# Grouped output norms of four recurrent mixers: row sums from ScalarE squares, and one reciprocal-root chain per unit

## The chip, the cores and the metric

The kernel runs on one core of a Trainium2 chip. The metric is the device time of one execution in microseconds. The engines are called as the profile calls them: PE (TensorE, matrix products), DVE (VectorE), ACT (ScalarE), POOL (GpSimd), and SP, which issues most DMAs. PSUM is the memory into which PE writes, SBUF the memory of the tiles.

## The reference

One layer of a decoder trunk on 2048 tokens of width 1024, in float32:

```
u = rmsnorm(x, norm_w);  proj = u @ w_in            # one projection for all mixers
y_a = gla(...)      # 4 heads, q and k of width 64, values of 128
y_b = mlstm(...)    # 4 heads of width 128
y_c = hgrn2(...)    # 4 heads of width 128
y_d = ssd(...)      # 8 heads of width 64, in 2 groups of 256
h = x + concat(y_a, y_b, y_c, y_d) @ w_out;  out = rmsnorm(h, final_norm_w)

grouped_rmsnorm(o) = o * rsqrt(mean(o*o over the group) + eps) * w    # ends each mixer
gla, hgrn2:  grouped_rmsnorm(o, per head) * silu(z)
mlstm:       grouped_rmsnorm(sigmoid(o_raw) * h, per head) * silu(z)
ssd:         grouped_rmsnorm(y * silu(z), 2 groups)
```

All four mixers are causal recurrences, computed in chunks. The change touches only how the last step of each mixer, the grouped norm with its gate, is computed.

## The kernel before

The tokens are worked through in two halves of 1024, and a half is eight chunks of 128 tokens, tiled with a chunk's tokens on the 128 partitions. In each half ten units follow one another: two pairs of GLA heads, two SSD groups, four HGRN2 heads and two pairs of mLSTM heads. After both halves a last stage multiplies by w_out.

Every unit has two parts. First its projections: `ps_c` (channels on the partitions) and `ps_t` (tokens on the partitions), both made in three matmuls of a split into a high and a low part (`uh`, `ul`, `hi`, `lo`). Then the recurrence, in a chain of dependent steps. For GLA and HGRN2 (`lin_unit`) these are decay levels, each of which multiplies `kb` and `qf` by a decay on DVE (L496, L497) and makes scores on PE (`ps_s`); then, for each of two groups of four chunks (`for g in range(2)`), a transpose of the keys (`ps_kt`, L567), its copy by ACT to SBUF (L569), the state update (`ps_u`, then DVE L577), and the output (`ps_o`). In SSD the recurrence steps chunk by chunk (L876 to L899). mLSTM has the same steps as the linear units, with exponentials made on ACT (L749, L757).

The Tile framework decides the order: each engine executes its instructions in one fixed order, which a list scheduler made at build time, and waits on semaphores. The scheduler puts matmuls of the following unit's projections (`ps_c`, `ps_t`) between the dependent steps of the recurrence. How many of them stand at a place is what this text calls the cover there.

Weights are loaded some groups ahead. `load_w` makes the high part on ACT (L228) and the low part on POOL (L230), two POOL instructions for a weight group. There are two buffers of each part, so the POOL pair starts when PE has done with the group before last.

The end of a unit before the change is, for each group of chunks and each head: ACT copies `ps_o` to SBUF (L590), ACT squares the copy (L602), DVE sums the rows (L604), eleven small DVE instructions form a reciprocal root with three Newton steps (`rsqrt`, L129), four DVE instructions multiply by the root and the gate `sz` (L595), DVE transposes (L613) and four DMAs store. SSD has its own version in `finish(g)`: squares with row sums in one ACT instruction (L843, with `accum_out`), the root, four scalings (L850); `finish(0)` is called in the middle of the chunk loop, after chunk 4.

The tile pool `t2k` (five buffers of 2 KB a partition) holds most intermediate tiles of this work; `small` holds the per-row factors.

Of the kernel before, what the change touches and what calls it, by code (L numbers as in the profile page):

```python
# [10 lines left out]
F32 = mybir.dt.float32  # L11
# [4 lines left out]
AF = mybir.ActivationFunctionType  # L16
ALU = mybir.AluOpType
# [4 lines left out]
P = 128  # L22
# [94 lines left out]
class Kernel:  # L117
# [11 lines left out]
    def rsqrt(self, x, w):  # L129

        nc, sm = self.nc, self.small
        y = sm.tile([P, 8], F32, tag="rs_y", name="rs_y")[:, :w]
        t = sm.tile([P, 8], F32, tag="rs_t", name="rs_t")[:, :w]
        nc.vector.tensor_scalar(out=t.bitcast(I32), in0=x.bitcast(I32), scalar1=1, scalar2=None, op0=ALU.logical_shift_right)
        nc.vector.tensor_scalar(out=y.bitcast(I32), in0=t.bitcast(I32), scalar1=-1.0, scalar2=float(0x5F3759DF), op0=ALU.mult, op1=ALU.add)
        for _ in range(3):
            nc.vector.scalar_tensor_tensor(out=t, in0=x, scalar=-0.5, in1=y, op0=ALU.mult, op1=ALU.mult)
            nc.vector.tensor_tensor(t, t, y, op=ALU.mult)
            nc.vector.scalar_tensor_tensor(out=y, in0=t, scalar=1.5, in1=y, op0=ALU.add, op1=ALU.mult)
        return y  # L140
# [276 lines left out]
    def lin_unit(self, nh, f, kb, qp, v, sz, car, eps, ycol, vt=None):  # L417
# [143 lines left out]
        if nh == 1:  # L561
            kr = flip_odd()
        for g in range(2):
            pt = self.psp.tile([P, 4, P], F32, tag="t", name="ps_kt")
# [23 lines left out]
            for h, po in enumerate(pos):  # L588
                ob = self.t2k().rearrange("p (c d) -> p c d", c=4)
                nc.scalar.copy(ob, po)  # L590
                rs2 = self.rs2[:, 4 * g:4 * g + 4]
                fac = self.rms(ob, eps, rs2)
                nc.vector.tensor_tensor(fac, fac, rs2, op=ALU.mult)
                for c in range(4):
                    nc.vector.scalar_tensor_tensor(out=ob[:, c], in0=ob[:, c], scalar=fac[:, c:c + 1], in1=sz(h, g)[:, c], op0=ALU.mult, op1=ALU.mult)  # L595
                self.store(ob, g, ycol + h * P)

    def rms(self, ob, eps, fac2):

        nc = self.nc  # L600
        sq = self.t2k().rearrange("p (c d) -> p c d", c=4)
        nc.scalar.activation(sq, ob, AF.Square)  # L602
        ss = self.small.tile([P, 8], F32, tag="f_ss", name="f_ss")[:, :4]
        nc.vector.tensor_reduce(out=ss, in_=sq, axis=AX.X, op=ALU.add)  # L604
        nc.vector.tensor_tensor(ss, ss, fac2, op=ALU.mult)
        nc.vector.tensor_scalar(out=ss, in0=ss, scalar1=1.0 / ob.shape[2], scalar2=eps, op0=ALU.mult, op1=ALU.add)
        return self.rsqrt(ss, 4)

# [114 lines left out]
    def mlstm(self, h):  # L723
# [17 lines left out]
        N = P + 1  # L741
        fac = self.small.tile([P, 8], F32, tag="m_fac", name="m_fac")
        for g in range(2):
            gs = slice(4 * g, 4 * g + 4)
# [32 lines left out]
            for u in range(2):  # L777
# [6 lines left out]
                nc.scalar.activation(rd[:, 2 * u:2 * u + 2].unsqueeze(2), po[:, :, P:N], AF.Abs)  # L784
            nc.vector.tensor_tensor(rd, rd, self.thr[:, gs, h], op=ALU.max)
            nc.vector.reciprocal(rd, rd)
            G = to[:, gs]
            nc.vector.scalar_tensor_tensor(out=G, in0=G, scalar=1.0, in1=ob, op0=ALU.add, op1=ALU.mult)
            rd2 = self.small.tile([P, 8], F32, tag="m_rd2", name="m_rd2")[:, :4]
            nc.vector.tensor_tensor(rd2, rd, rd, op=ALU.mult)  # L790
            nc.vector.tensor_tensor(rd, rd, self.rs[:, gs], op=ALU.mult)
            nc.vector.tensor_tensor(rd, rd, self.rms(G, 4 * EPS, rd2), op=ALU.mult)
        return to, fac
# [24 lines left out]
    def ssd(self, q):  # L818
# [18 lines left out]
        dD = self.dd[:, h4].unsqueeze(2).to_broadcast([P, 4, 64])  # L837
        def finish(g):
            yb = szs[g]
            ss = self.small.tile([P, 8], F32, tag="s_ss", name="s_ss")[:, :4]  # L840
            junk = self.t2k()[:, :256]
            for c in range(4):
                nc.scalar.activation(junk, yb[:, c], AF.Square, accum_out=ss[:, c:c + 1])  # L843
            gs = slice(4 * g, 4 * g + 4)
            nc.vector.tensor_tensor(ss, ss, self.rs2[:, gs], op=ALU.mult)
            nc.vector.tensor_scalar(out=ss, in0=ss, scalar1=1.0 / 256, scalar2=256 * EPS, op0=ALU.mult, op1=ALU.add)
            rs = self.rsqrt(ss, 4)
            nc.vector.tensor_tensor(rs, rs, self.rs[:, gs], op=ALU.mult)
            for c in range(4):
                nc.vector.tensor_scalar(out=yb[:, c], in0=yb[:, c], scalar1=rs[:, c:c + 1], scalar2=None, op0=ALU.mult)  # L850
            for j in range(2):
                self.store(yb[:, :, j * P:(j + 1) * P], g, 1536 + 256 * q + j * P)

        for g in range(2):
            yb = szs[g]
            for u in range(2):
# [3 lines left out]
                for j in range(2):  # L860
# [38 lines left out]
                    nc.vector.tensor_tensor(H, H, pu, op=ALU.add)  # L899
                    if cc == 4:  # L900
                        finish(0)
        finish(1)


# [239 lines left out]
```

## Time and profile before

| | |
|---|---|
| median of three runs | 2236.55 us (2234.35 to 2238.48) |
| the profiled execution | 2236.62 us, span 2234.8 us |
| PE busy | 2113.7 us, 95% |
| DVE busy | 1395.2 us, 62% |
| ACT busy | 821.5 us, 37% |
| POOL busy | 382.7 us, 17% |
| mean granted clock of PE | 0.983 |

A row of the timeline gives the start, the duration, the engine and the line, then the output and input tiles with their shapes, a count, and in brackets the idle time of the engine just before with the instruction that ended it. Releasers are inferred: when the one named had long been done, it was another.

### The profile page before, as it was taken

The numbers are of one execution on the slowest core, as the hardware profiler recorded it, in microseconds if no ns is written. First come the engines' busy times: TensorE is split into PE (matmuls) and PEld (weight loads), VectorE is DVE, ScalarE is ACT, GpSimd is POOL, SyncE is SP. The second block draws the span as 40 slices with busy tenths as digits, with TensorE's granted clock in tenths as the row PEclk, the third lists the DMA queues.
The fourth block names the chain that finished last, engine by engine and source line by source line (L and its number), as shares of the span: only waits on it lengthen the run. The fifth ranks groups of instructions, "written<-read, shape, count | busy, mean of one in ns | idle before, by whom it ended". The sixth has DMA issues, their size and how long they took to land.

```text
span 2234.8 us, 35049 instructions
## 1 busy us (share of the span) xinstructions
PE 2113.7 (95%) x13758; PEld 1888.7 (85%) x13758; DVE 1395.2 (62%) x3325; ACT 821.5 (37%) x1763; POOL 382.7 (17%) x283
## 2 busy tenths in 40 slices
PE   8899999989999999998989899999999999999998
PEld 7888788878889998997978788888899998788887
DVE  3674878767667676636677876776676566532332
ACT  6633332344434334454323223443343334321211
POOL 3212122320111111121211222211111210000000
PEclk9999999999999999999999989999999999999999
DMA  7111212221111132420202222211121215432321
GB/s 235 56 34 44 58 47 66 69 48 48 49 49 39 49 84 106 126 75 22 58 24 62 69 46 76 54 36 43 45 76 49 56 48 175 160 111 78 113 71 48
DMA packets 186149, 156.66 MB, mean 70 GB/s; under 512 B 141944, under 2 KB 154344, under 8 KB 178688
## 3 DMA queue, kind: packets, MB, share of 16 engines
q1 hardware_dynamic: 179504, 135.02, 21.2%
q10 hardware_dynamic: 6480, 19.40, 2.4%
q8 instruction: 108, 1.77, 0.3%
q14 instruction: 57, 0.47, 0.1%
HBM read 129.11 MB, written 25.27 MB: 69 GB/s over the span
## 4 chain that ended last, share of the span: by engine, by line
PE 75%; DVE 16%; ACT 4%; DMA 2%; issue 2%; POOL 0%; SPq 0%; ACTq 0%; DVEq 0%
PE ps_t L123 26%; PE ps_c L123 19%; PE ps_out L123 15%; PE ps_o L123 6%; PE ps_s L123 4%; PE ps_u L123 2%; PE ps_g L123 2%; DVE t2k L884 2%; DVE kb L496 2%; DVE qf L497 1%; DVE xc L717 1%; DMA ST<-w_out 1%; DMA t2k<-xT 1%; DVE st L766 1%; DMA ab<-rows 1%
## 5 line engine op out<-in xcount | busy, mean ns | idle before, releaser
L123 PE MATMUL ps_t<-hi,uh 128*128 128x256 f32 x1920 | 546.5, 285 | 0.0
L123 PE MATMUL ps_t<-hi,ul 128*128 128x256 f32 x1920 | 546.0, 284 | 0.0
L123 PE MATMUL ps_t<-lo,uh 128*128 128x256 f32 x1920 | 545.1, 284 | 0.0
L230 POOL TENSOR_TENSOR lo<-raw,hi 128x1024 fp32r<-128x1024 f32 (+1 forms) x118 | 294.4, 2515 | 950.2 <-ACT hi L228 917.3
L123 PEld LDWEIGHTS ps_t<-lo,uh 128*128 128x128 f32 x1920 | 369.8, 193 | 0.9
L123 PEld LDWEIGHTS ps_t<-hi,uh 128*128 128x128 f32 x1920 | 369.6, 193 | 1.0
L123 PEld LDWEIGHTS ps_t<-hi,ul 128*128 128x128 f32 x1920 | 369.5, 192 | 1.0 <-issue 0.9
L123 PE MATMUL ps_c<-uh,hi 128*128 128x512 f32 x896 | 357.9, 400 | 7.4 <-ACT uh L155 7.4
L123 PE MATMUL ps_c<-uh,lo 128*128 128x512 f32 x896 | 358.6, 400 | 0.0
L123 PE MATMUL ps_c<-ul,hi 128*128 128x512 f32 x896 | 357.7, 399 | 0.0
L123 PEld LDWEIGHTS ps_c<-uh,hi 128*128 128x128 f32 x896 | 171.5, 191 | 40.4 <-ACT uh L155 7.8
L123 PEld LDWEIGHTS ps_c<-ul,hi 128*128 128x128 f32 x896 | 171.6, 191 | 34.7 <-DVE ul L156 0.5
L123 PEld LDWEIGHTS ps_c<-uh,lo 128*128 128x128 f32 x896 | 171.1, 191 | 33.5
L228 ACT CAST hi<-raw 128x512 fp32r<-128x512 f32 (+1 forms) x236 | 134.6, 626 | 59.6 <-issue 33.2
L956 DVE TENSOR_TENSOR o_sz<-o_sz,ps_out 128x512 f32<-128x512 f32 (+1 forms) x33 | 22.1, 671 | 130.5 <-PE ps_out L123 127.9
L123 PE MATMUL ps_out<-woh,o_qp 128*128 128x512 f32 x288 | 94.0, 394 | 0.0
L281 ACT ACTIVATE v<-ps_t,ss 128x128 f32<-128x128 f32 x128 | 39.7, 361 | 129.3 <-PE ps_t L123 129.0
L276 ACT ACTIVATE sz<-ps_t,ss 128x128 f32<-128x128 f32 (+1 forms) x160 | 53.2, 387 | 65.2 <-PE ps_t L123 58.1
L123 PE MATMUL ps_out<-woh,o_v 128*128 128x512 f32 (+1 forms) x213 | 75.4, 389 | 0.0
L277 DVE SCALAR_TENSOR_TENSOR sz<-sz,ps_t 128x256 f32<-128x256 f32 (+1 forms) x80 | 37.5, 469 | 60.7 <-ACT sz L276 60.4
L497 DVE TENSOR_TENSOR qf<-qf,pl 128x512 f32<-128x512 f32 x72 | 61.0, 847 | 21.6 <-ACT t2k L472 12.1
L496 DVE TENSOR_TENSOR kb<-kb,pl 128x512 f32<-128x512 f32 x72 | 67.9, 942 | 10.3 <-PE ps_s L123 9.4
(367 smaller groups left out, 3793.1 us busy)
## 6 DMA issues: line engine op xcount, KB each, us to landing
raw<-w SPq DMA_DIRECT2D x59, 1024.0 KB, 4.8
y<-t2k SPq DMA_DIRECT2D x256, 64.0 KB, 2.0
t2k<-y SPq DMA_DIRECT2D x64, 256.0 KB, 3.5
t2k<-xT SPq DMA_DIRECT2D x32, 256.0 KB, 3.6
ab<-rows SPq DMA_DIRECT2D x16, 512.0 KB, 5.0
o_sz<-x ACTq DMA_DIRECT2D x16, 512.0 KB, 4.5
o_f<-x SPq DMA_DIRECT2D x12, 512.0 KB, 5.3
mb<-rows SPq DMA_DIRECT2D x8, 512.0 KB, 3.6
```

Of the source, the lines that this page charges most:

```text
L123: self.nc.tensor.matmul(out, l, r, start=start, stop=stop, skip_group_check=shared)
L228: nc.scalar.copy(hi[:, k0:k1], raw[:, k0:k1])
L230: nc.gpsimd.tensor_tensor(lo[:, k0:k1], raw[:, k0:k1], hi[:, k0:k1].bitcast(F32), op=ALU.subtract)
L276: nc.scalar.activation(out[:, j], ps[:, j], AF.Tanh, scale=self.rsh[:, t + j:t + j + 1])
L277: nc.vector.scalar_tensor_tensor(out=out, in0=out, scalar=1.0, in1=ps, op0=ALU.add, op1=ALU.mult)
L281: self.nc.scalar.activation(out[:, j], ps[:, j], AF.Identity, scale=sc[:, t + j:t + j + 1])
L496: nc.vector.tensor_tensor(kv[:, :, 0], kv[:, :, 0], pv[:, :, 1:2].to_broadcast([P, n, b]), op=ALU.mult)
L497: nc.vector.tensor_tensor(qv[:, :, 1], qv[:, :, 1], pv[:, :, 0:1].to_broadcast([P, n, b]), op=ALU.mult)
L717: nc.vector.scalar_tensor_tensor(out=acc, in0=raw[:, k:k + TH], scalar=cw[k], in1=acc, op0=ALU.mult, op1=ALU.add)
L766: nc.vector.tensor_copy(st[:, 0, :N], car)
L884: nc.vector.scalar_tensor_tensor(out=L[:, h], in0=ab[:, h, j * C:(j + 1) * C], scalar=self.acs[:, cc, 4 * q + h:4 * q + h + 1], in1=self.c ...
L956: nc.vector.tensor_tensor(xt[:, ns], xt[:, ns], ps, op=ALU.add)
```

## The change

In the linear units `squares` reads `ps_o` in PSUM with four ACT instructions, each of which squares the 128 columns of a chunk and writes their row sum into `ss`. One DVE instruction multiplies the gate tile `sz` by `ps_o`, and with that `ps_o` is free. When both groups are through, one root chain serves all eight chunks of all heads of the unit (8 or 16 columns instead of 4), and `scale_rows` multiplies each chunk by its factor. The copy L590, the square L602, the reduction L604 and the four multiplications by root and gate L595 are gone. mLSTM keeps its gated tile `G`, takes its row sums with `squares`, and makes all factors once per head. SSD calls `squares` after each group and `finish` once, after both; the call in the middle of its chunk loop is gone.

```diff
--- before.py
+++ after.py
@@ -129,8 +129,8 @@
     def rsqrt(self, x, w):
 
         nc, sm = self.nc, self.small
-        y = sm.tile([P, 8], F32, tag="rs_y", name="rs_y")[:, :w]
-        t = sm.tile([P, 8], F32, tag="rs_t", name="rs_t")[:, :w]
+        y = sm.tile([P, 16], F32, tag="rs_y", name="rs_y")[:, :w]
+        t = sm.tile([P, 16], F32, tag="rs_t", name="rs_t", bufs=1)[:, :w]
         nc.vector.tensor_scalar(out=t.bitcast(I32), in0=x.bitcast(I32), scalar1=1, scalar2=None, op0=ALU.logical_shift_right)
         nc.vector.tensor_scalar(out=y.bitcast(I32), in0=t.bitcast(I32), scalar1=-1.0, scalar2=float(0x5F3759DF), op0=ALU.mult, op1=ALU.add)
         for _ in range(3):
@@ -560,6 +560,7 @@
                     nc.scalar.copy(ST[0:64, :, 64:128], ps[0:64])
         if nh == 1:
             kr = flip_odd()
+        ss = self.small.tile([P, 16], F32, tag="f_ss", name="f_ss")[:, :8 * nh]
         for g in range(2):
             pt = self.psp.tile([P, 4, P], F32, tag="t", name="ps_kt")
             for c in range(4):
@@ -586,25 +587,33 @@
                 for h, po in enumerate(pos):
                     self.mm(po[:, c], qf[rows[h], cc * C:(cc + 1) * C], st[rows[h], c, :P], start=False, stop=c == 3, shared=True)
             for h, po in enumerate(pos):
-                ob = self.t2k().rearrange("p (c d) -> p c d", c=4)
-                nc.scalar.copy(ob, po)
-                rs2 = self.rs2[:, 4 * g:4 * g + 4]
-                fac = self.rms(ob, eps, rs2)
-                nc.vector.tensor_tensor(fac, fac, rs2, op=ALU.mult)
-                for c in range(4):
-                    nc.vector.scalar_tensor_tensor(out=ob[:, c], in0=ob[:, c], scalar=fac[:, c:c + 1], in1=sz(h, g)[:, c], op0=ALU.mult, op1=ALU.mult)
-                self.store(ob, g, ycol + h * P)
-
-    def rms(self, ob, eps, fac2):
-
-        nc = self.nc
-        sq = self.t2k().rearrange("p (c d) -> p c d", c=4)
-        nc.scalar.activation(sq, ob, AF.Square)
-        ss = self.small.tile([P, 8], F32, tag="f_ss", name="f_ss")[:, :4]
-        nc.vector.tensor_reduce(out=ss, in_=sq, axis=AX.X, op=ALU.add)
-        nc.vector.tensor_tensor(ss, ss, fac2, op=ALU.mult)
-        nc.vector.tensor_scalar(out=ss, in0=ss, scalar1=1.0 / ob.shape[2], scalar2=eps, op0=ALU.mult, op1=ALU.add)
-        return self.rsqrt(ss, 4)
+                self.squares(po, ss[:, 8 * h + 4 * g:8 * h + 4 * g + 4])
+                nc.vector.tensor_tensor(sz(h, g), sz(h, g), po, op=ALU.mult)
+        fac = self.rms(ss, P, eps, self.rs2, nh)
+        f3 = fac.rearrange("p (h c) -> p h c", h=nh)
+        nc.vector.tensor_tensor(f3, f3, self.rs2[:, None].to_broadcast([P, nh, NC]), op=ALU.mult)
+        for g in range(2):
+            for h in range(nh):
+                self.scale_rows(sz(h, g), fac[:, 8 * h + 4 * g:8 * h + 4 * g + 4])
+                self.store(sz(h, g), g, ycol + h * P)
+
+    def squares(self, ob, ss):
+
+        junk = self.t2k()[:, :ob.shape[2]]
+        for c in range(4):
+            self.nc.scalar.activation(junk, ob[:, c], AF.Square, accum_out=ss[:, c:c + 1])
+
+    def scale_rows(self, ob, fac):
+        for c in range(4):
+            self.nc.vector.tensor_scalar(out=ob[:, c], in0=ob[:, c], scalar1=fac[:, c:c + 1], scalar2=None, op0=ALU.mult)
+
+    def rms(self, ss, n, eps, fac2, nh=1):
+
+        nc = self.nc
+        s3 = ss.rearrange("p (h c) -> p h c", h=nh)
+        nc.vector.tensor_tensor(s3, s3, fac2[:, None].to_broadcast([P, nh, NC]), op=ALU.mult)
+        nc.vector.tensor_scalar(out=ss, in0=ss, scalar1=1.0 / n, scalar2=eps, op0=ALU.mult, op1=ALU.add)
+        return self.rsqrt(ss, 8 * nh)
 
     def store(self, ob, g, ycol):
 
@@ -740,6 +749,7 @@
         nc.sync.dma_start(mb, self.rows[h:h + 1, :].broadcast_to([P, TH]))
         N = P + 1
         fac = self.small.tile([P, 8], F32, tag="m_fac", name="m_fac")
+        ss = self.small.tile([P, 16], F32, tag="f_ss", name="f_ss")[:, :8]
         for g in range(2):
             gs = slice(4 * g, 4 * g + 4)
             mb3 = mb[:, g * 512:(g + 1) * 512].rearrange("p (c t) -> p c t", c=4)
@@ -782,14 +792,15 @@
                     self.mm(po[:, j], ib[:, c], st[:, c, :N], start=False, stop=True)
                 nc.scalar.copy(ob[:, 2 * u:2 * u + 2], po[:, :, :P])
                 nc.scalar.activation(rd[:, 2 * u:2 * u + 2].unsqueeze(2), po[:, :, P:N], AF.Abs)
-            nc.vector.tensor_tensor(rd, rd, self.thr[:, gs, h], op=ALU.max)
-            nc.vector.reciprocal(rd, rd)
             G = to[:, gs]
             nc.vector.scalar_tensor_tensor(out=G, in0=G, scalar=1.0, in1=ob, op0=ALU.add, op1=ALU.mult)
-            rd2 = self.small.tile([P, 8], F32, tag="m_rd2", name="m_rd2")[:, :4]
-            nc.vector.tensor_tensor(rd2, rd, rd, op=ALU.mult)
-            nc.vector.tensor_tensor(rd, rd, self.rs[:, gs], op=ALU.mult)
-            nc.vector.tensor_tensor(rd, rd, self.rms(G, 4 * EPS, rd2), op=ALU.mult)
+            self.squares(G, ss[:, gs])
+        nc.vector.tensor_tensor(fac, fac, self.thr[:, :, h], op=ALU.max)
+        nc.vector.reciprocal(fac, fac)
+        rd2 = self.small.tile([P, 8], F32, tag="m_rd2", name="m_rd2")
+        nc.vector.tensor_tensor(rd2, fac, fac, op=ALU.mult)
+        nc.vector.tensor_tensor(fac, fac, self.rs, op=ALU.mult)
+        nc.vector.tensor_tensor(fac, fac, self.rms(ss, P, 4 * EPS, rd2), op=ALU.mult)
         return to, fac
 
     def mlstm_pair(self, p):
@@ -835,21 +846,15 @@
         H = self.hst[:, q]
         h4 = slice(4 * q, 4 * q + 4)
         dD = self.dd[:, h4].unsqueeze(2).to_broadcast([P, 4, 64])
-        def finish(g):
-            yb = szs[g]
-            ss = self.small.tile([P, 8], F32, tag="s_ss", name="s_ss")[:, :4]
-            junk = self.t2k()[:, :256]
-            for c in range(4):
-                nc.scalar.activation(junk, yb[:, c], AF.Square, accum_out=ss[:, c:c + 1])
-            gs = slice(4 * g, 4 * g + 4)
-            nc.vector.tensor_tensor(ss, ss, self.rs2[:, gs], op=ALU.mult)
-            nc.vector.tensor_scalar(out=ss, in0=ss, scalar1=1.0 / 256, scalar2=256 * EPS, op0=ALU.mult, op1=ALU.add)
-            rs = self.rsqrt(ss, 4)
-            nc.vector.tensor_tensor(rs, rs, self.rs[:, gs], op=ALU.mult)
-            for c in range(4):
-                nc.vector.tensor_scalar(out=yb[:, c], in0=yb[:, c], scalar1=rs[:, c:c + 1], scalar2=None, op0=ALU.mult)
-            for j in range(2):
-                self.store(yb[:, :, j * P:(j + 1) * P], g, 1536 + 256 * q + j * P)
+        ss = self.small.tile([P, 16], F32, tag="f_ss", name="f_ss")[:, :8]
+
+        def finish():
+            rs = self.rms(ss, 256, 256 * EPS, self.rs2)
+            nc.vector.tensor_tensor(rs, rs, self.rs, op=ALU.mult)
+            for g in range(2):
+                self.scale_rows(szs[g], rs[:, 4 * g:4 * g + 4])
+                for j in range(2):
+                    self.store(szs[g][:, :, j * P:(j + 1) * P], g, 1536 + 256 * q + j * P)
 
         for g in range(2):
             yb = szs[g]
@@ -897,9 +902,8 @@
                     nc.gpsimd.tensor_tensor(yb[:, c], y1, yb[:, c], op=ALU.mult)
                     nc.vector.tensor_tensor(v4(H), v4(H), self.el[:, h4, cc:cc + 1].to_broadcast([P, 4, 64]), op=ALU.mult)
                     nc.vector.tensor_tensor(H, H, pu, op=ALU.add)
-                    if cc == 4:
-                        finish(0)
-        finish(1)
+            self.squares(yb, ss[:, 4 * g:4 * g + 4])
+        finish()
 
 
     def flat(self, tag, n, dtype=F32):
```

The order in which the engines execute follows from the code and the scheduler. Three places show it.

PE at the second group of chunks of the second GLA pair; `ps_kt` is the transpose of the keys, `ps_c` the projection of the unit that follows, `ps_u` the state update. Before:

```order
1057 L123 MATMUL ps_o<-st,qf 128x128 x8
1058 L567 MATMUL ps_kt<-cf,kb 128x128 x4
1059 L123 MATMUL ps_c<-uh,hi 128x512
...
1128 L123 MATMUL ps_c<-uh,hi 128x512
1129 L123 MATMUL ps_u<-o_v,t2k 64x128 x8
1130 L123 MATMUL ps_o<-o_v,ST_93 128x128 x4
```

and now:

```order
1057 L123 MATMUL ps_o<-st,qf 128x128 x8
1058 L568 MATMUL ps_kt<-cf,kb 128x128 x4
1059 L123 MATMUL ps_c<-uh,hi 128x512
...
1067 L123 MATMUL ps_c<-uh,lo 128x512
1068 L123 MATMUL ps_u<-o_v,t2k 64x128 x8
1069 L123 MATMUL ps_o<-o_v,ST_93 128x128 x4
```

Between the transpose and the state update stand 9 projection matmuls (1059 to 1067) where 70 stood (1059 to 1128).

ACT at the same place; `t2k<-ps_kt` is the copy that the state update reads, once for each group of chunks. Before:

```order
113 L569 COPY t2k<-ps_kt 128x512
114 L590 COPY t2k<-ps_o 128x512
115 L602 ACTIVATE t2k<-t2k 128x512
...
121 L228 CAST hi<-raw 128x512 x2
122 L714 ACTIVATE v<-craw,par 128x512
123 L569 COPY t2k<-ps_kt 128x512
```

and now:

```order
109 L570 COPY t2k<-ps_kt 128x512
110 L604 ACTIVATE t2k,f_ss<-ps_o 128x128 x8
111 L570 COPY t2k<-ps_kt 128x512
112 L723 ACTIVATE xc<-craw,par 128x512
113 L728 ACTIVATE th<-xc 128x1024
114 L604 ACTIVATE t2k,f_ss<-ps_o 128x128 x8
```

The eight squares of the first group stand directly ahead of the key copy of the second, and the convolution's activations (L714 before, L723 now) have moved behind it.

DVE in the chunk loop of the first SSD group, between the chunks 5 and 6; `s_ss` and `rs_y` belong to the norm, L876 to L899 to the chunks. Before:

```order
424 L139 SCALAR_TENSOR_TENSOR rs_y<-rs_t,rs_y 128x4
425 L848 TENSOR_TENSOR rs_y<-rs_y,ss 128x4
426 L850 TENSOR_SCALAR sz<-sz,rs_y 128x256 x4
427 L613 STREAM_TRANSPOSE t2k<-sz 128x512 x2
428 L876 TENSOR_TENSOR t2k<-ps_xt,g_sp 128x256
429 L877 TENSOR_TENSOR t2k<-ps_xt,dd 128x256
430 L884 SCALAR_TENSOR_TENSOR t2k<-ab,g_cs,cf 128x128 x2
```

and now:

```order
297 L903 TENSOR_TENSOR hst<-hst,g_el 128x256
298 L881 TENSOR_TENSOR t2k<-ps_xt,g_sp 128x256
299 L904 TENSOR_TENSOR hst<-hst,ps_u 128x256
300 L882 TENSOR_TENSOR t2k<-ps_xt,dd 128x256
301 L889 SCALAR_TENSOR_TENSOR t2k<-ab,g_cs,cf 128x128 x3
```

The norm that stood ahead of the chunk's own DVE work is no longer there; a chunk now follows directly on the one before.

## Rows read from the trace of the kernel before

**Rows 1.** The page, busy time, share of the span and instructions of each engine.

```profile
PE 2113.7 (95%) x13758; PEld 1888.7 (85%) x13758; DVE 1395.2 (62%) x3325; ACT 821.5 (37%) x1763; POOL 382.7 (17%) x283
```

**Rows 2.** One stretch: length, busy time (count) of each engine, granted clock, DMA share, GB/s.

```profile
250.70:254.10 3.40, 3.40 (x23) 3.07 (x24) 2.15 (x7) 0.01 (x1) 0.00 (x0) 0.50 0.41 61
```

**Rows 3.** The core's span and its mean granted clock.

```profile
core 0: 2234.8 us, clock 0.983
```

**Rows 4.** Waits of PE: who waited for what, total us, times, longest us.

```profile
PE ps_o L123 <- DVE t2k L886: 27.1, 14, 3.8
...
PE ps_u L123 <- DVE rs_y L135: 10.0, 7, 1.5
PE ps_u L123 <- ACT t2k L569: 8.8, 4, 4.0
...
PE ps_o L123 <- DVE halo L715: 5.7, 2, 2.9
PE ps_o L123 <- DVE st L577: 2.9, 2, 1.5
```

**Rows 5.** Timeline of PE: five matmuls that ended an idle time.

```profile
250.60 1.92 PE L123 MATMUL ps_u<-o_v,t2k 128*64 128x128 f32 x16 [3.94 <-ACT t2k L569]
...
351.56 0.41 PE L123 MATMUL ps_o<-t2k 128*128 128x64 f32 x2 [2.86 <-DVE halo L715]
...
499.49 0.35 PE L123 MATMUL ps_s<-qf,t2k 128*128 128x128 f32 x1 [1.40 <-DVE qf L497]
...
666.35 0.35 PE L123 MATMUL ps_s<-qf,t2k 128*128 128x128 f32 x1 [0.96 <-DVE qf L497]
...
784.94 0.35 PE L123 MATMUL ps_u<-v,t2k 128*128 128x129 f32 x1 [1.54 <-DVE rs_y L135]
```

**Rows 6.** Timeline of DVE and ACT ahead of the first two idle times of rows 5.

```profile
249.26 0.81 ACT L714 ACTIVATE v<-craw,par 128x512 f32<-128x512 f32 x1 [7.96 <-DVE craw L713]
...
339.99 0.15 DVE L845 TENSOR_TENSOR s_ss<-s_ss,ss 128x4 f32<-128x4 f32 x1
...
346.65 1.31 DVE L613 STREAM_TRANSPOSE t2k<-sz 128x512 f32<-128x512 f32 x2
```

**Rows 7.** Timeline: POOL's low parts, and DVE beside and after them.

```profile
295.04 4.75 POOL L230 TENSOR_TENSOR lo<-raw,hi 128x1024 fp32r<-128x1024 f32 x2 [19.28 <-ACT hi L228]
...
295.45 4.76 DVE L884 SCALAR_TENSOR_TENSOR t2k<-ab,g_cs,cf 128x128 f32<-128x128 f32 x3
...
331.67 4.93 POOL L230 TENSOR_TENSOR lo<-raw,hi 128x1024 fp32r<-128x1024 f32 x2 [3.13 <-ACT hi L228]
...
499.26 2.85 DVE L496 TENSOR_TENSOR kb<-kb,pl 128x512 f32<-128x512 f32 x1
...
503.97 0.69 DVE L496 TENSOR_TENSOR kb<-kb,pl 128x512 f32<-128x512 f32 x1 [0.45 <-ACT t2k L439]
```

**Rows 8.** Groups of instructions by line and shape: busy us, mean ns | idle before.

```profile
L604 DVE TENSOR_REDUCE f_ss<-t2k 128x4 f32<-128x512 f32 x48 | 32.6, 679 | 16.8 <-ACT t2k L602 16.7
...
L850 DVE TENSOR_SCALAR sz<-sz,rs_y 128x256 f32<-128x256 f32 x32 | 9.1, 350 | 0.3
...
L281 ACT ACTIVATE v<-ps_t,ss 128x128 f32<-128x128 f32 x128 | 39.7, 361 | 129.3 <-PE ps_t L123 129.0
L569 ACT COPY t2k<-ps_kt 128x512 f32<-128x512 f32 x24 | 14.0, 581 | 8.2 <-PE ps_kt L567 4.4 <-DVE t2k L613 3.7
...
L602 ACT ACTIVATE t2k<-sz 128x512 f32<-128x512 f32 x16 | 10.1, 632 | 20.4 <-DVE sz L788 20.1 <-DVE m_fac L786 0.3
...
L843 ACT ACTIVATION_READ_ACCUMULATOR t2k<-sz 128x1 f32 x32 | 6.0, 188 | 0.0
```

**Rows 9.** Timeline of ACT: two of the four squares with row sums of an SSD group.

```profile
333.96 0.40 ACT L843 ACTIVATE t2k<-sz 128x256 f32<-128x256 f32 x1
...
334.49 0.42 ACT L843 ACTIVATE t2k<-sz 128x256 f32<-128x256 f32 x1
```

**Rows 10.** Stretch with projection matmuls of ps_c alone: PE busy (count), PEld, DVE, ACT, clock.

```profile
240.00:246.00 6.00, 6.00 (x28) 4.99 (x27) 0.00 (x0) 0.00 (x0) 1.00 0.25 36
```

## The prediction

> **What bounds the kernel now.** I read the page's busy times first. PE works 2113.7 us of a span of 2234.8 us, DVE 1395.2 and ACT 821.5 [rows 1, 3]. The change takes no matmul away, so it can win or lose only in PE's idle time. This is what the waits of PE list, some 112 us in all; five lines of that list concern what the change touches [rows 4]. Third comes the timeline around single idle times, to see which engine is late there, and why.
>
> - In the GLA pairs the update `ps_u` of the second group waits 3.94 us [rows 5] for ACT's copy of the keys. ACT had been idle for 7.96 us, because the activation queued ahead of that copy waited for a DVE convolution [rows 6], which on DVE stood between the instructions of the norm. So here the norm is late. All waits of this kind are 8.8 us, and 2.9 us more stand at the first pair (`st` L577) [rows 4].
> - In SSD, chunks wait 27.1 and 5.7 us [rows 4]. One cause is the norm in mid-loop: on DVE it runs from 339.99 to 347.96 [rows 6], and the next chunk's first matmul then waits 2.86 us [rows 5]. The other is POOL: from 295.04 a pair of low parts takes 4.75 us and three L884 beside it take 4.76 [rows 7]; the wait behind it is the longest of the line, 3.8 us [rows 4].
> - In HGRN2 the levels wait for L496, L497 and the copy of their result. I count eight such gaps in a half, 10.0 us together, the first and last of them 1.40 and 0.96 [rows 5]. There, too, POOL runs beside DVE: L496 took 2.85 us at 499.26 and 0.69 us at 503.97 [rows 7].
> - In mLSTM `ps_u` waits for the roots on DVE, 10.0 us in seven waits [rows 4]; an eighth of about 1.5 us I add from the timeline (1.54 is the longest [rows 5]). 11.5 us.
>
> The clock matters a little. Its mean is 0.983 [rows 3], which is some 22 stretches of 3.4 us at 0.5, or 1.2 GHz, instead of 2.4 (0.017 x 2235 / 0.5 / 3.4). One begins at the very end of the 3.94 us gap [rows 2, 5]. PE is then busy all the time at half its speed, so one costs at most 1.7 us; I take 1, as matmuls limited otherwise lose less.
>
> **The change part by part.** What leaves DVE is large, over 100 us: 48 reductions of 679 ns are 32.6 us [rows 8], and most small root instructions go, since 56 chains of 4 columns become 24 of 8 or 16. None of it counts by itself, DVE being idle for a third of the span. What counts is where it stood.
>
> ACT gains 192 squares of 128 columns. No such row exists. The lower bound is a plain activation of 128 columns, 0.36 us with the readout hidden (L281), the upper one the spacing of squares with sums of 256 columns, 0.53 us, readout included [rows 8, 9]. I take 0.45: 0.53 less 128 columns at (632 - 361)/384 = 0.7 ns [rows 8], rounded up.
>
> The Trainium skill, page "ScalarE: Activation LUTs" (section "What ACT_TABLE_LOAD costs"), puts a start of about 0.28 us on an ACTIVATE (with its bias in a tile) and 0.83 ns on a column, which speaks against cutting one square of 512 into four. By it a square would be 0.39 us plus the readout of 0.19, 0.58 us, 0.13 more than I take; some 74 squares stand on PE's path below (4 x 8 in GLA, 8 x 4 in mLSTM, some 10 in HGRN2), and the sum would come out at 2231. The rows show instructions of one line starting closer together than their length [rows 9], so I stay with 0.45.
>
> *GLA.* PE's cover between transpose and `ps_u` falls from 70 projection matmuls to 9, and ACT does 8 squares ahead of the key copy. So the copy ends 8 x 0.45 + 0.58 (L569 [rows 8]) = 4.2 us after the output of the first group. PE spends about 0.3 us on the transposes and 9 x 0.22 = 2.0 us on the cover (28 in 6.0 us [rows 10]). The gap is 1.9 us, four times 7.6 against 11.7 now: -4.1 us (1.2 to 2.5 each with the bounds of a square: -6.9 to -1.7).
>
> *SSD.* The norm in mid-loop goes with its wait, and the chunks close up. The POOL pair at the first chunk stays where it was, 3.8 us four times (two groups, two halves), 15.0 of the 32.8. Of the other 17.8 the chunk loop keeps little, except that the pair now at 331.67 [rows 7], which PE's long cover hides, comes to lie beside the sixth chunk of the first group, with a cover of 22 to 23 matmuls (5.0 us) against 4.9 us of POOL and the rest of the chunk: 2.4 us. With 0.3 for the second group that is 5.4 us for both halves. -12.4 us (from -17.8, nothing left, to -2.6, two full collisions of 3.8 in each half).
>
> *HGRN2.* The order of matmuls shifts by a few dozen, and with it where a weight group ends and POOL starts. Laying the 4.9 us of a pair over the new order I get 0.3 for the first head, 2.5 for the second, 0.5 for the third and 2.25 for the fourth: 5.5 instead of 10.0 in a half. At the change of groups the key copy stands behind one or two squares, with 4 to 7 matmuls of cover instead of 29: 0.4 us a head. For both halves 14.2 against 20.0: -5.8 us (-15 if no pair collides, +4 if all do as before).
>
> *mLSTM.* Here the change costs. Four squares of 0.45 replace one of 0.63 (L602 [rows 8]) and stand between the exponentials, so these end 1.2 us later, and the cover ahead of `ps_u` falls from 15 projection matmuls to 7. The norm chain on DVE that made the wait is gone, but kt still comes after the gated tile and the decays. I make it 1.45 us before `ps_u` and 1.1 before the output, eight times 20.4 against 11.5: +8.9 us (0 to +12).
>
> *The tail of a unit.* One chain and the scalings for 8 or 16 chunks come after the recurrence; stores are not needed before the last stage, and PE has the next unit's projections. I put it at nothing; without that cover it would be about 5 us a unit. Scalings by `tensor_scalar` take 0.35 us for 256 columns (L850 [rows 8]).
>
> The Trainium skill, page "SBUF — State Buffer" (section "Who interferes with whom"), says that a DVE instruction with two SBUF inputs contends with a POOL one that reads SBUF, and that a `tensor_scalar` can too, in a mode with two ports; the first to start blocks the other. Rows 7 agree on the first. By the second, scalings would be stretched to a POOL pair's 4.9 us, on DVE behind PE's cover, and the sum would not move.
>
> *Sum.* -4.1 - 12.4 - 5.8 + 8.9 = -13.4 us. Two falls of the clock follow gaps that vanish (3.94 and 2.86 us) in each half, but new gaps may bring others: -2 us. The profiled execution took 2236.6 us, its span and 1.8 around it, the same as the median. 2236.6 - 15.4 = 2221.
>
> **Rivals.**
>
> 1. *No change.* POOL's pairs go on colliding in HGRN2 at their new places, squares cost 0.53. HGRN2 then +4, GLA -1.7, mLSTM +12, SSD -12.4, clock -2: 2237. For it: every cover became shorter; against it: the order shows most pairs away from the levels.
> 2. *Slower: the POOL pairs land on the chains.* Seven pairs a half change their place. One that meets a chunk or a level chain costs up to 3.8 us (the SSD wait [rows 4]). Four more a half than I count are 8 x 3.8 = 30 us: 2221 + 30 = 2251. It decides from about four in both halves on, where -15 is used up. For it: covers of 5 us barely hide a pair of 4.9. Against it: the pairs follow the end of a weight group, which I could place.
> 3. *Much faster.* mLSTM's gap doesn't grow, since the cover that the scheduler took away was not needed: +0 instead of +8.9, and all four clock stretches go: 2221 - 8.9 - 2 = 2210.
>
> **Chances.** Forecast 0.50 (its own range 2213 to 2229), much faster 0.20, no change 0.17, slower 0.13. The range that leaves out about 2 in 10 is 2205 to 2243. A measurement of this kernel can tell 0.2%, 4.5 us, from no change. Faster: the forecast and rival 3 nearly whole and a little of rival 1, 0.72. Same: most of rival 1, 0.15. Slower: 0.13.
>
> **What would show it.** In the waits of PE after: the L886 line down to some 20 us with its longest still 3.8; `rs_y` gone from mLSTM, in its place waits on ACT's exponentials or the key factor of 1 to 1.5 us each; `ps_u` on the key copy at about 1.9 us four times in GLA; DVE's busy time near 1270 us and ACT's near 865 us; squares of 128 columns spaced 0.45 us. I am wrong if PE's idle time is not less by some 13 us, or if L496, L497 or L884 stand beside POOL at more places than now.

## The result and the profile after

The changed kernel takes 2199.52 us (2198.02 to 2206.66), the one before 2236.64: a ratio of 0.984, 95% interval 0.9825 to 0.9855. It is 37 us faster. The sign was right, the size was not: 15 us were forecast, and 2199.5 lies below the range that was given. The profiled execution answers to [rows 1, 3]; first the busy times of its page, then its cores:

```profile
PE 2103.6 (96%) x13758; PEld 1879.6 (86%) x13758; DVE 1298.6 (59%) x2829; ACT 834.4 (38%) x2067; POOL 381.3 (17%) x283
```

```profile
core 0: 2196.2 us, clock 0.989
```

The span is 38.6 us shorter. I added up PE's idle times in both traces: 113.4 us before, 84.9 after, so 28.5 us are waits that went. The other 10.1 are PE's own busy time, 2113.7 before: the same 13758 matmuls ran faster, as PE stood at 1.2 GHz for 49.2 us instead of 78.1. Waits of PE after, to be laid beside [rows 4]:

```profile
PE ps_o L123 <- DVE t2k L891: 19.5, 12, 3.7
PE ps_s L123 <- DVE kb L496: 14.8, 6, 3.5
PE ps_s L123 <- DVE qf L497: 10.9, 8, 2.0
PE ps_u L123 <- DVE t2k L774: 9.7, 7, 1.4
...
PE ps_s L123 <- ACT t2k L439: 4.6, 4, 1.3
...
PE ps_u L123 <- ACT t2k L570: 1.4, 6, 0.3
```

The long waits for the key copy (L569, 8.8 us) and for `st` L577 have left the list; of SSD's 32.8 us 19.5 stay. mLSTM waits as long as before, under another name. By place, over both halves and in us:

| | idle before | after | measured | forecast |
|---|---|---|---|---|
| GLA, change of groups | 11.7 | 0.9 | -10.8 | -4.1 |
| SSD, chunk loop | 32.8 | 19.5 | -13.3 | -12.4 |
| HGRN2, levels and groups | 20.0 | 16.0 | -4.0 | -5.8 |
| mLSTM, ahead of `ps_u` | 10.0 | 9.7 | -0.3 | +8.9 |
| PE busy (clock) | 2113.7 | 2103.6 | -10.1 | -2 |

The rest is under 1 us; it stands at the start and ahead of the last stage. Next the timeline after at the second group of the second GLA pair, ACT's first two and last squares, the key copy and PE's `ps_u`, which waited 3.94 us [rows 5]:

```profile
227.07 0.28 ACT L604 ACTIVATE t2k<-ps_o 128x128 f32<-128x128 f32 x1 [4.43 <-PE ps_o L123]
227.25 0.19 ACT L604 ACTIVATION_READ_ACCUMULATOR t2k<-ps_o 128x1 f32 x1
227.34 0.27 ACT L604 ACTIVATE t2k<-ps_o 128x128 f32<-128x128 f32 x1
...
228.84 0.32 ACT L604 ACTIVATE t2k<-ps_o 128x128 f32<-128x128 f32 x1
...
229.09 0.64 ACT L570 COPY t2k<-ps_kt 128x512 f32<-128x512 f32 x1
229.77 1.09 PE L123 MATMUL ps_u<-o_v,t2k 128*64 128x128 f32 x16 [0.17 <-ACT t2k L570]
```

In GLA the squares start every 0.25 us, readout included. Eight are 2.0 us, with the copy 2.7, and PE's transposes and nine matmuls hide nearly all of it. And here is where this unit's norm went, in the same trace, POOL and then DVE:

```profile
240.65 4.74 POOL L230 TENSOR_TENSOR lo<-raw,hi 128x1024 fp32r<-128x1024 f32 x2 [7.16 <-ACT hi L228]
```

```profile
240.11 5.36 DVE L608 TENSOR_SCALAR o_sz<-o_sz,rs_y 128x128 f32<-128x128 f32 x5
```

Five scalings take 5.36 us beside the POOL pair. So the norm still meets a pair, but nobody waits: the unit's last `ps_o` is done, and PE has the next projections.

### The profile page after: what moved, and what is told of

The parts are those of the page before. It is cut to its first block, busy times and chain, and to the rows that moved or that the text cites. A ratio compares the mean times of both kernels' runs of the same rounds, so it can differ in the third digit from the quotient of the medians.

```text
span 2196.2 us, 34886 instructions
## 1 busy us (share of the span) xinstructions
PE 2103.6 (96%) x13758; PEld 1879.6 (86%) x13758; DVE 1298.6 (59%) x2829; ACT 834.4 (38%) x2067; POOL 381.3 (17%) x283
## 5 line engine op out<-in xcount | busy, mean ns | idle before, releaser
L496 DVE TENSOR_TENSOR kb<-kb,pl 128x512 f32<-128x512 f32 x72 | 60.7, 844 | 9.4 <-PE ps_s L123 9.4
```

The lines of the kernel that those rows point to most:

```text
L496: nc.vector.tensor_tensor(kv[:, :, 0], kv[:, :, 0], pv[:, :, 1:2].to_broadcast([P, n, b]), op=ALU.mult)
```

## The experiments

Theory A, from the prediction: the norm's place on DVE costs, and its removal from the chains is the gain. Theory B: the gain follows the DVE time that is freed. Theory L, set against A once the parts were measured: a wait arises where a POOL pair blocks DVE on a chain that PE waits for, each colliding DVE instruction until the POOL instruction beside it ends. Times are medians; the kernel before stood at 2235 to 2237 beside them.

**The parts alone.** The changed kernel with two of its three parts put back as they were.

The edits in words:

```diff
 # e1: only ssd() as changed; lin_unit() and mlstm() as before
 # e2: only lin_unit() as changed; ssd() and mlstm() as before
 # e3: only mlstm() as changed; lin_unit() and ssd() as before
```

> Only the SSD part of the change; the linear units and mLSTM as before. Theory A (a part is worth the idle places of PE that it removes, plus the clock stretches that began in them): SSD's idle time falls from 32.8 to about 19 us over both halves, four half-clock stretches of about 1.3 us go: 2236.6 - 13.6 - 5 = about 2218. Theory B (the gain follows the DVE time that is freed, 97 us for 38 us in the whole change): four of eight root chains go, some 10 us of DVE, so about 4 us: 2232.

> Only the linear units (GLA and HGRN2) changed; SSD and mLSTM as before. Theory A: GLA's two boundary waits go (10.8 us of idle time over both halves), HGRN2's levels lose 4.5, and the four stretches at half clock that began at GLA's boundaries go (5 us): about 2216. Theory B: some 75 us of the freed DVE time stands here, so 29 us: 2207.

> Only mLSTM changed; the linear units and SSD as before. Theory A: its eight waits ahead of ps_u stay 1.35 to 1.45 us with another instruction named (the key product on DVE instead of the root), and no second wait appears: 2236, within 2 us. Theory B: 15 to 20 us of DVE time go here, so 6 to 8 us: 2229. The prediction's own step (+8.9 us) would give 2245.

Measured 2213.79 (ratio 0.9897, 0.9883 to 0.9912), 2214.91 (0.9904, 0.9888 to 0.992) and 2237.07 (1.0002, 0.9993 to 1.0012): -23, -22 and nothing. Theory B falls: DVE's busy time fell by 5, 65 and 17 us for these. That A comes within 5 us each time says less: its numbers had been read off the waits of the changed kernel. The parts sum to 44 us, 7 more than the whole.

**Squares made twice.**

```diff
 # inside "for c in range(4)" of squares; dump is a spare piece of the tile of junk
+            if ob.shape[2] == P:
+                self.nc.scalar.activation(junk, ob[:, c], AF.Square, accum_out=dump[:, c:c + 1])
             self.nc.scalar.activation(junk, ob[:, c], AF.Square, accum_out=ss[:, c:c + 1])
```

> The changed kernel with every 128-column square with its row sum made twice on ACT (linear units and mLSTM; 192 more instructions, some 50 us of ACT). If my prediction failed because a square costs 0.25 to 0.31 us and not 0.45, the double one (0.5 to 0.6) brings the missing waits: a second wait of about 1 us per half head in mLSTM, ahead of the output, whose cover is unchanged (8 of them, +8 us), 0.4 us a head in HGRN2 (+3), and in GLA little, as the order there has 18 to 25 matmuls of cover instead of 9: about 2211. If ACT's squares are off the path altogether, 2200.

Measured 2198.04 (0.9828, 0.9813 to 0.9843): 192 more squares cost nothing. The order says why. The scheduler knew of them: in GLA's second pair it put 18 matmuls ahead of `ps_u` instead of 9 (PE waited less than 0.25 us there, as in the changed kernel), and in mLSTM only three of the eight squares stand ahead of the exponential that the output needs. So the run doesn't show what a slower square would have cost in the changed order; it shows that at these places the scheduler made the cover as long as it expected the wait to be.

**DVE work put back at the end of the units.**

```diff
-        nc.vector.transpose(yt.rearrange("p (c d) -> p c d", c=4), ob)
+        for _ in range(3):
+            nc.vector.transpose(yt.rearrange("p (c d) -> p c d", c=4), ob)
```

> The changed kernel with each of the 64 transpositions ahead of the stores made three times (128 more of 0.70 us, 90 us of DVE, about what the change freed, all at the end of the units). Theory A (only what stands on a chain that PE waits for counts): 2200, within 5 us. Rival B (the freed DVE time was the gain): 2235.

Measured 2206.13 (0.987, 0.9856 to 0.9885), 6.6 us over the changed kernel, with DVE busy for 83 us more: a little over A's margin, far from B.

**POOL's instructions cut.**

```diff
-        for k0, k1 in ((0, 4), (4, 8)):
+        for k0, k1 in tuple((k, k + 1) for k in range(8)):          # e5
+        for k0, k1 in ((0, 2), (2, 4), (4, 6), (6, 8)):             # e6
             nc.gpsimd.tensor_tensor(lo[:, k0:k1], raw[:, k0:k1], hi[:, k0:k1].bitcast(F32), op=ALU.subtract)
```

> The changed kernel with POOL's low parts (L230) made in eight instructions of 256 columns (of 0.6 to 0.7 us) instead of two of 1024 (2.4 us); the order on PE and DVE is the same but for a few rows. Theory L (a DVE instruction that collides waits for the end of the POOL instruction beside it, so for one piece at most): the four waits of 3.7 us at SSD's first chunks become about 1.5, those of 3.5 in the GLA levels about 1, HGRN2's and mLSTM's shrink by half, and with them go some half-clock stretches: idle time 85 to about 60 us, 2165 to 2180. Rival R (DVE and POOL share a port for as long as the whole POOL work lasts, whatever its cuts): no change, 2199.

> The same with four instructions of 512 columns (about 1.25 us each). Theory L: about half of the gain of the eight pieces, near 2187, as a colliding DVE instruction waits up to 1.25 us instead of up to 2.4. Rival R: 2199.

Measured 2158.18 with eight (0.9658, 0.9643 to 0.9672) and 2197.62 with four (0.9833, 0.9819 to 0.9848). Eight beat what L gave; four missed it, and their time alone is the one that R gave. PE's order is the same in all three kernels but for five matmuls, so this is the effect of the cut by itself. The timeline at SSD's first chunk, eight pieces and then four, tells both; with two, three L884 took 4.76 us [rows 7]:

```profile
282.44 5.77 POOL L230 TENSOR_TENSOR lo<-raw,hi 128x256 fp32r<-128x256 f32 x8 [9.23 <-ACT hi L228]
...
283.59 1.99 DVE L889 SCALAR_TENSOR_TENSOR t2k<-ab,g_cs,cf 128x128 f32<-128x128 f32 x3
```

```profile
288.68 5.15 POOL L230 TENSOR_TENSOR lo<-raw,hi 128x512 fp32r<-128x512 f32 x4 [9.21 <-ACT hi L228]
...
290.38 3.60 DVE L889 SCALAR_TENSOR_TENSOR t2k<-ab,g_cs,cf 128x128 f32<-128x128 f32 x3
```

Three instructions took nearly three pieces' time: 3.60 us at 1.29 a piece, 1.99 at 0.72. With two pieces two of the three wait, with four all three and one before them, so halving the pieces gains little here, PE waiting 3.30 us instead of 3.75; that is what I had left out. A shared rate, the rival, would not follow the cut. Of the whole, PE's idle time fell from 84.9 to 76.9 us with four, but PE stood at 1.2 GHz for 66.2 us instead of 49.2, and its busy time rose by 7.1; why it stood there longer stays open. With eight the idle time fell to 52.2. L's details held only in part there: SSD's first waits came to 1.1 us (1.5 given), the longest in GLA's levels to 2.5 (1), and mLSTM's stayed, 9.0 us in seven waits, where L gave half.

**The low parts on DVE.**

```diff
-            nc.gpsimd.tensor_tensor(lo[:, k0:k1], ...)
+            nc.vector.tensor_tensor(lo[:, k0:k1], ...)     # e7, e12 (four pieces): changed kernel; e9: kernel before
```

> The changed kernel with the low parts made by DVE in place of POOL (two instructions of 1024 columns, by the row of a DVE instruction of this size with two inputs in SBUF 1.28 us each, 151 us of DVE in all). No collision is left. Theory L: a chain that met a POOL pair of 4.9 us now meets at most 2.6 us of DVE work, so SSD's first waits go from 3.7 to about 1.5 and the time to about 2185. Rival B (DVE's load counts): 151 us more of it at the rate of 38 us for 97 would give 2258.

> The kernel before with the low parts made by DVE in place of POOL, nothing else. If the change gains by taking the norm off the path, independent of POOL, the low parts on DVE are worth the same 70 us here as in the changed kernel, and the change 36 on top: about 2165. Rival C (the change gained because less DVE work stands beside POOL's pairs): without collisions both kernels are nearly alike, 2130 to 2140.

> The changed kernel with the low parts on DVE in four instructions of 512 columns (0.68 us each) instead of two of 1024 (1.28). An instruction that comes ready behind one waits half as long; the waits left are few (30 us, of which 6 at the start): 2124 to 2129.

Measured 2128.95 (0.9529, 0.9513 to 0.9545), 2134.09 (0.9544, 0.9522 to 0.9565) and 2129.88 (0.9528, 0.9509 to 0.9546). The first is the fastest version run, 70 us under the changed kernel. B (2258) is out, but L missed too, having given 2185: of the 73 us between the two traces, 55 are waits, far more than the halving that L put, and 17 are PE's busy time, with 12.5 us at 1.2 GHz instead of 49.2. The second speaks for one cause: with its norms where they were, but no POOL pairs, the kernel before is within 5 us of the changed one without them. Its waits of PE, in which no root and no norm is left to speak of:

```profile
PE ps_o L123 <- DVE t2k L886: 2.5, 6, 0.7
...
PE ps_u L123 <- ACT t2k L569: 0.7, 2, 0.4
...
PE ps_o L123 <- DVE st L577: 0.5, 2, 0.3
```

The third, with pieces half as long, gained nothing more. The other case of the second run, the norm's place by itself, gave 2165. Theory A, as it stood, fell. One reservation holds for these runs: the scheduler knew of DVE's new work and laid the order anew. Some 3100 of the 13758 matmuls stand at another place than in the kernel before; at the second GLA pair 81 cover the wait instead of 70, in the first mLSTM head 17 instead of 15. The 11 more are 2.4 us at the rate of [rows 10], of a wait of 3.94. So a part of what went there may be longer cover.

**SSD's norm moved, alone.**

```diff
-                    if cc == 4:
-                        finish(0)
+        finish(0)
         finish(1)
```

> The kernel before with one edit: SSD's finish(0) is called after the chunk loop, ahead of finish(1), with its own chain and squares as before. If the place of the norm on DVE is what costs, this alone gives most of the 23 us of the run with only SSD changed: 2214 to 2219. If the length (two chains instead of one, more instructions) matters, little is gained: 2230 or more.

Measured 2230.58 (0.9979, 0.9968 to 0.999), 5 us, not 20. The time is also the one given for the other case, the length of the norm; the trace says where it went. The waits of the mid-loop norm were gone as expected, but in the second SSD group the shifted order put POOL on the chunks, PE then waiting 3.84 us at 443.32:

```profile
432.72 2.40 POOL L230 TENSOR_TENSOR lo<-raw,hi 128x1024 fp32r<-128x1024 f32 x1 [4.93 <-ACT hi L228]
...
433.33 2.06 DVE L898 TENSOR_TENSOR hst<-hst,g_el 128x256 f32<-128x256 f32 x1
...
436.32 3.06 DVE L884 SCALAR_TENSOR_TENSOR t2k<-ab,g_cs,cf 128x128 f32<-128x128 f32 x2
436.78 2.45 POOL L230 TENSOR_TENSOR lo<-raw,hi 128x1024 fp32r<-128x1024 f32 x1
...
443.32 0.48 PE L123 MATMUL ps_o<-t2k 128*128 128x64 f32 x1 [3.84 <-DVE t2k L886]
```

The run with only SSD changed had 0.51 us there.

**A chain per group, with POOL's pairs and without.**

```diff
 # inside "for g in range(2)" of lin_unit, in place of the one chain behind the loop:
+            fac = self.rms(ss[:, 4 * nh * g:4 * nh * (g + 1)], P, eps, r4, nh, 4)
...
+                self.scale_rows(sz(h, g), fac[:, 4 * h:4 * h + 4])
                 self.store(sz(h, g), g, ycol + h * P)
```

> The changed kernel with one root chain, the scalings and the stores per group of chunks inside the loop of the linear units (12 chains more), the squares and the gates as changed. If the place of the norm matters in GLA too, the chain of the first group stands on DVE ahead of the state of the second again: a wait of 1 to 2 us at each of the four GLA boundaries, with a half-clock stretch behind some: 2205 to 2212. If the copy, the reduction and the four gated products were the cost, 2200.

> The changed kernel with a root chain per group in the linear units, as in the run of that name (2219, 20 us over the changed kernel), and the low parts on DVE. Theory L (a wait needs a POOL pair that blocks DVE on the chain; the norm alone is covered): within 5 us of the changed kernel with the low parts on DVE, 2129 to 2134. Theory A (the norm's place is enough): its four GLA waits of 2 us and their clock stretches stay: 2140 or more.

Measured 2219.41 (0.9928, 0.9908 to 0.9948), and without the pairs 2130.10 (0.9526, 0.9512 to 0.954). With the pairs the place costs 20 us, more than the 5 to 12 that were given; without them it costs 1, as L gave, here too in an order that was laid anew. The first of the two, at the first GLA pair, POOL, DVE and PE in one timeline:

```profile
138.84 4.74 POOL L230 TENSOR_TENSOR lo<-raw,hi 128x1024 fp32r<-128x1024 f32 x2 [26.82 <-ACT hi L228]
138.87 2.40 DVE L138 TENSOR_TENSOR rs_t<-rs_t,rs_y 128x8 f32<-128x8 f32 x1
141.31 2.29 DVE L139 SCALAR_TENSOR_TENSOR rs_y<-rs_t,rs_y 128x8 f32<-128x8 f32 x1
...
144.44 1.07 DVE L608 TENSOR_SCALAR o_sz<-o_sz,rs_y 128x128 f32<-128x128 f32 x5
...
147.79 0.38 PE L123 MATMUL ps_o<-st,qf 64*128 64x128 f32 x2 [2.10 <-DVE st L578]
```

Two instructions of 0.17 us last 2.40 and 2.29, and PE waits 2.10 for the state that stands behind the chain.

**The kernel before with eight pieces, and with short chains.** The edits: the cut of e5 in the kernel before; `range(3)` to `range(1)` in `rsqrt`.

> The kernel before with POOL's low parts in eight instructions of 256 columns. Theory L: the change is worth little once POOL's pairs don't block for long, so this lies 5 to 15 us over the changed kernel with the same pieces (2158): 2163 to 2173. Theory A: the change keeps its 37 us: 2195.

> The kernel before with one Newton step in every reciprocal root instead of three (the roots are less precise), 6 of 11 small DVE instructions less in each of 56 chains of the output norms, some 65 us of DVE. Theory L: the length of the norm is covered, so only the chance of where POOL's pairs fall moves: 2230 to 2240. If the length of the norm counts, as much DVE time went from the linear units for 22 us: 2215.

Measured 2180.73 (0.9766, 0.9742 to 0.979), 23 us over the changed kernel with the same cut, between the two theories; PE's order is that of the kernel before but for five matmuls. The trace shows the middle way, DVE and PE at the second GLA pair:

```profile
235.13 0.66 DVE L137 SCALAR_TENSOR_TENSOR rs_t<-f_ss,rs_y 128x4 f32<-128x4 f32 x1
235.82 0.66 DVE L138 TENSOR_TENSOR rs_t<-rs_t,rs_y 128x4 f32<-128x4 f32 x1
236.52 0.67 DVE L139 SCALAR_TENSOR_TENSOR rs_y<-rs_t,rs_y 128x4 f32<-128x4 f32 x1
...
245.52 0.33 PE L123 MATMUL ps_u<-o_v,t2k 128*64 128x128 f32 x2 [3.37 <-ACT t2k L569]
```

A chain of small instructions pays one piece for each of them: beside the eight pieces DVE lost 3.7 us, beside the pair 4.2. So cutting POOL's work frees chunks and levels but not a norm. Short chains gave 2225.35 (0.996, 0.9948 to 0.9972), 10 us, half-way between the cases. The trace is of the slowest of its ten runs (2234.87), in which PE stood at 1.2 GHz for 89.9 us; PE's idle time there, 104.9 us, is still 8.5 less than before. GLA's waits at the change of groups came to 4.6 us instead of 11.7, with shorter covers (45 matmuls instead of 70 at the second pair), and SSD's to 34.0 instead of 32.8. So the length counts in GLA, with the pairs in place, but the run doesn't part it from where the pairs fall.

## Why the prediction was wrong

**What bounds the kernel** was read rightly: PE's waits, with the norm and POOL as the late ones. But I took them for two causes. In GLA and SSD they were one, as the kernel before shows at the first GLA pair, POOL and then DVE, with the same four products at 148.91 in the clear:

```profile
139.13 4.83 POOL L230 TENSOR_TENSOR lo<-raw,hi 128x1024 fp32r<-128x1024 f32 x2 [25.23 <-ACT hi L228]
```

```profile
139.28 5.35 DVE L595 SCALAR_TENSOR_TENSOR t2k<-t2k,rs_y,o_sz 128x128 f32<-128x128 f32 x4
...
148.91 1.14 DVE L595 SCALAR_TENSOR_TENSOR t2k<-t2k,rs_y,o_sz 128x128 f32<-128x128 f32 x4
```

The norm stood on DVE ahead of the state, the pair blocked it for 4.2 us, and PE waited 1.45. The two waits that the prediction laid to the norm alone are of the same kind. Here is DVE ahead of the 3.94 us in GLA, beside the pair at 239.36, then ahead of the 2.86 us in SSD, beside the pair at 331.67 [rows 7] that I had called hidden, and last the same copy in the clear:

```profile
239.45 2.33 DVE L715 COPY halo<-craw 128x3 f32<-128x3 f32 x1
...
241.88 2.25 DVE L138 TENSOR_TENSOR rs_t<-rs_t,rs_y 128x4 f32<-128x4 f32 x1
```

```profile
334.26 2.37 DVE L715 COPY halo<-craw 128x3 f32<-128x3 f32 x1
...
351.33 0.16 DVE L715 COPY halo<-craw 128x3 f32<-128x3 f32 x1
```

Against the same instructions in the clear, DVE lost 4.2 us ahead of the first and 2.8 ahead of the second; the other waits of over 1 us that left GLA and SSD had 2.5 to 4.3 us of such blocking ahead of them. Take away the pairs (2134) or the place (2199.5, and 2219.4 with it put back) and nearly all of them are gone.

**The step that failed** is the pricing of new waits where the cover became shorter, in the parts on GLA and mLSTM, and with it the clock's term in the sum. These three are 6.7, 9.2 and 8.1 us off, which is the whole of the 23 us that the sum missed of the span; SSD and HGRN2 were off by 0.9 and 1.8, in opposite directions.

- GLA: 4 x 1.9 us were put, 0.9 in all came. The mechanism was right and the term mis-sized: a square takes 0.25 us there, under my lower bound of 0.36, since I read a lone activation's length for a spacing. With it the same sum gives 8 x 0.25 + 0.6 - 2.3 = 0.3, which is what the first pair waited. But 0.25 us holds for GLA alone. The squares of HGRN2, from PSUM as well, follow one another every 0.40 us, and those of mLSTM, from SBUF, every 0.43 where four stand together, close to my 0.45; why GLA's come closer is not shown. First the groups after, from PSUM and from SBUF, then two squares of HGRN2 and two of mLSTM:

```profile
L604 ACT ACTIVATE t2k<-ps_o 128x128 f32<-128x128 f32 x128 | 34.5, 284 | 62.7 <-PE ps_o L123 61.4
L604 ACT ACTIVATION_READ_ACCUMULATOR t2k<-ps_o 128x1 f32 x128 | 26.7, 209 | 0.0
...
L604 ACT ACTIVATE t2k<-sz 128x128 f32<-128x128 f32 x64 | 19.3, 301 | 20.5 <-DVE sz L796 20.1
```

```profile
507.24 0.28 ACT L604 ACTIVATE t2k<-ps_o 128x128 f32<-128x128 f32 x1
...
507.64 0.28 ACT L604 ACTIVATE t2k<-ps_o 128x128 f32<-128x128 f32 x1
...
770.11 0.31 ACT L604 ACTIVATE t2k<-sz 128x128 f32<-128x128 f32 x1 [0.68 <-DVE sz L796]
...
770.54 0.31 ACT L604 ACTIVATE t2k<-sz 128x128 f32<-128x128 f32 x1
```

  The estimate weighed there, 0.58 us for a square by the Trainium skill, page "ScalarE: Activation LUTs" (section "What ACT_TABLE_LOAD costs"), was further off. It left out what the same section states, that ACTIVATEs that follow one another overlap by some 0.09 us, and it counted the readout in full; the trace agrees that they overlap, with squares of 0.28 us and readouts of 0.21 behind them, 0.25 to 0.40 us from square to square.
- mLSTM: +8.9 us were put, -0.3 came. Waits before were seven, of 10.0 us together; the eighth that I added isn't in the trace. The wait ahead of `ps_u` I had right in its number (1.45 forecast, 1.41 measured); the second, ahead of the output, did not appear. Timeline after, DVE, ACT and PE:

```profile
706.29 1.91 DVE L776 COPY st<-mst 128x129 f32<-128x129 f32 x1 [0.40 <-PE ps_o L123]
...
708.83 0.31 ACT L604 ACTIVATE t2k<-sz 128x128 f32<-128x128 f32 x1 [2.10 <-DVE sz L796]
...
710.31 0.62 ACT L759 ACTIVATE t2k<-t2k 128x512 f32<-128x512 f32 x1
...
710.60 1.13 PE L123 MATMUL ps_u<-v,t2k 128*128 128x129 f32 x8 [1.41 <-DVE t2k L774]
...
711.80 0.68 PE L123 MATMUL ps_o<-v,t2k 128*128 128x129 f32 x4
```

  Three squares, not four, stand ahead of the exponential L759, and a square with the small exponential L767 behind it takes 0.59 us. The 1.41 us are again POOL's: the copy of 1.91 us (0.23 in the clear) starts the group. So it did in the kernel before, 1.91 us at 724.39 ahead of the first wait, where I had blamed the norm's roots; that is why the wait stayed when the roots left. Without the pairs the wait is gone, with two matmuls more of cover.
- The clock: -2 us were put, -10.1 came. PE ran at 1.2 GHz for 28.9 us less; that is 0.35 us for each. I had named two stretches in a half, and eight or nine as long as that of [rows 2] went, among them those that began at 151.7 and 452.1 us, behind waits of 1.45 and 2.69 us that are gone.

**What held.** SSD came to -13.3 against -12.4, with its first chunks at 3.7 as forecast; in part that is luck, since the waits that went had a pair ahead of them that I had not seen. HGRN2 came to -4.0 against -5.8, but by errors that cancel: hardly a wait at the change of groups (0.24 us at one head in each half, where 0.4 was put at each), and a pair on the first head that I had cleared (2.6 us of waits against 0.3). The tail of a unit cost nothing, with 5.36 us of scalings in it. On those the Trainium skill, page "SBUF — State Buffer" (section "Who interferes with whom"), which lets a `tensor_scalar` contend with POOL too, agrees with the trace: 5.36 us for five beside the pair, 1.07 in the clear. Of the rivals, the third named mLSTM and the clock rightly and still gave 2210; the second, pairs landing on chains, happened in the run with only `finish(0)` moved.

**What stays open.** By how much the length of a norm counts when a pair meets it (2225 with one Newton step). How much of the gain without pairs is owed to the covers that the scheduler laid anew; the runs that leave the order as it was (eight pieces) cut the worth of the change only from 37 to 23 us. And the 37 us rest partly on where pairs fall in this order: the three parts alone sum to 44.

## What to carry to other kernels

Look at what blocks an engine before you price what stands on it: a chain that the scheduler has covered can still wait for what the scheduler doesn't reckon with, here another engine's instruction that holds DVE. Where two explanations stand at one wait, cross them, each with and without the other; the four kernels here (2199.5 and 2219.4 with the pairs, 2129.0 and 2130.1 without) say more than any sum, though an edit that the scheduler sees moves the order too, and wants a run beside it that leaves the order alone. And read the spacing of instructions that follow one another, not the length of one.

## What the runs showed of the hardware

- A DVE instruction with two inputs in SBUF, begun beside POOL's subtraction, waited for the end of the POOL instruction then running, whatever its own size: 0.17 us became 2.4 beside pieces of 1024 columns and 0.66 beside 256. Small copies and `tensor_scalar` were blocked too. Sums and products with one of their two inputs in PSUM were not: L893 of the kernel before took 0.42 us beside a pair and in the clear.
- POOL needs 4.75 us for the two of 1024 columns, 5.15 for four of 512, 5.77 for eight of 256. DVE made one of 1024 in 1.22 us, and its busy time was still lower with this work (1272.8 us) than without (1298.6). In the changed kernel the DVE instructions that began beside a pair took some 142 us more than the same ones in the clear, about what the 118 subtractions cost DVE (144 us).
- Squares of 128 columns with row sums follow one another every 0.25 us from PSUM in GLA and every 0.40 in HGRN2, every 0.43 from SBUF; of 256 columns from SBUF every 0.53 [rows 9].
